# Scale and shift of k tile 0 by one-column matmuls, and silu of c spread by diagonal matmuls, in the prologue of a transformer block

## The chip, the cores and the metric

One Trainium2 chip, of which the kernel uses one core. The metric is the device time of one execution in microseconds (us), the median of three runs.

## The reference

One encoder block on 256 tokens of width 2048, in float32. A modulation vector of 9 x 2048 numbers is computed from c. It scales, shifts and gates three sublayers: a SwiGLU feed-forward (width 5632), a two-headed-group attention, and a second feed-forward.

```
def modulate(n, shift, scale):
    return n * (1 + scale[:, None, :]) + shift[:, None, :]

mod = jax.nn.silu(c) @ w_ada[l] + b_ada[l]            # 2048 x 18432
sh1, sc1, gt1, sh2, sc2, gt2, sh3, sc3, gt3 = jnp.split(mod, N_MOD, axis=-1)
f = swiglu(modulate(rms_norm(h, g_ffn1[l]), sh1, sc1), w1_gate[l], w1_up[l], w1_down[l])
h = h + 0.5 * gt1[:, None, :] * f
... attention with sh2, sc2, gt2, then a second feed-forward with sh3, sc3, gt3
```

## The kernel before

Activations are kept transposed: 16 k tiles (`h[k]`, 128 features by 256 tokens). The weights stream through once, in units of 128x1024 float32 (512 KB, tile `rw`, four buffers). ScalarE rounds a unit to float32r (`hiw`, line 83), VectorE subtracts to get the rest (`low`, line 90), and TensorE makes each product from three matmuls, hi by hi, hi by low and low by hi (lines 222 to 224). The normalised activation of a k tile is split in the same way into `nh` (line 307, ScalarE) and `nl` (line 310, VectorE), after line 304 (VectorE, `nt`) has multiplied h by the row's scale and by 1/rms.

The modulation numbers are made on VectorE. For 128 of them, `ada_use` (line 195) multiplies two 128x1024 units of `w_ada` (tile `ra`) by `cb`, which is silu(c) spread over all 128 partitions, and sums along the row. So one k tile's scale and shift take four such instructions. `acc` holds the results.

The program is written in a fixed order (a manual schedule), and each engine takes its instructions in that order. All loads are issued by SyncE, at most eight under way.

The first stage, `up_start`, runs k tiles 0, 1 and 2 (K1 = 3). Before each k tile, `before1` writes the work that it needs: the four `ada_use`, the norm (lines 304, 307, 310), and the hi and low of two weight units. Each k tile then has 24 matmuls of 512 columns into eight PSUM banks (tile `pa`). From then on `up_pass` takes the rest of the feed-forward, with one weight unit to each twelve matmuls (tile `pu`), and the remaining modulation work is given out at a set rate per unit.

Ahead of `up_start` stand: the load of c, spread over the partitions by the DMA (`cb`, two halves, lines 466 and 468), and of small vectors (`vec`); tanh and one VectorE operation on each half of `cb` for silu (lines 489 and 490); the loads of `ra` for k tile 0, then of x (line 480), then of weights and of `ra` for k tiles 1 and 2; the squares of x (line 503, ScalarE, four of 128x1024); sixteen matmuls of 256 columns with a matrix of ones, which sum the squares over the partitions (line 505, tile `pstat`, plain float32); and 1/rms from that sum (lines 244 to 252, `rs`).

Of the kernel before, what the change touches and what calls it, by code (L numbers as in the profile page):

```python
# [9 lines left out]
F32 = mybir.dt.float32  # L10
F32R = mybir.dt.float32r
AF = mybir.ActivationFunctionType
ALU = mybir.AluOpType
AX = mybir.AxisListType

P = 128
S = 256
D = 2048
KT = D // P
# [6 lines left out]
CW = 1024  # L26
# [123 lines left out]
def build(tc, a):  # L150
    nc = tc.nc
    with ExitStack() as ctx:
        cp = ctx.enter_context(tc.tile_pool(name="cp", bufs=1))
# [4 lines left out]
        def bank(nm):  # L158
            return pb.tile([P, 512], F32, tag="b", name=nm)
# [4 lines left out]
        fl = Flow(tc, a, wp, srcs)  # L164

        ones = cp.tile([P, P], F32, name="ones")
# [3 lines left out]
        ident = cp.tile([P, P], F32, name="ident")  # L170
        make_identity(nc, ident)

        G1, GO, BA = 0, 48, 80
        vec = cp.tile([P, 224], F32, name="vec")
        cb = cp.tile([P, D], F32, name="cb")
        h4 = [cp.tile([P, 4, S], F32, tag=f"h{k}", name=f"h{k}") for k in range(4)]
        h = [h4[k // 4][:, k % 4, :] for k in range(KT)]
        acc = cp.tile([P, 9, 2, KT], F32, name="acc")
# [3 lines left out]
        gsc = cp.tile([P, 3, KT], F32, name="gsc")  # L182
        gin = cp.tile([P, 3, KT], F32, name="gin")
        gat = cp.tile([P, 2, KT], F32, name="gat")

        def ada_use(j, k, b, raw):
            if j in (1, 4, 7):
                scale, init = gsc[:, j // 3, k : k + 1], gin[:, j // 3, k : k + 1]
            elif j in (2, 8):
                scale, init = 0.25, gat[:, j // 3 // 2, k : k + 1]  # L190
            else:
                scale, init = 0.5, vec[:, BA + j * KT + k : BA + j * KT + k + 1]
            if b == 1:
                init = acc[:, j, 0, k : k + 1]
            nc.vector.tensor_tensor_reduce(  # L195
                out=raw, in0=raw, in1=cb[:, b * CW : (b + 1) * CW], scale=scale, scalar=init,
                op0=ALU.mult, op1=ALU.add, accum_out=acc[:, j, b, k : k + 1])
            if b == 1:
                modded.add((j, k))

        modded = set()
# [34 lines left out]
        def ln_exp_set():  # L236
            nc.scalar.preload_act_table_set("natural_log_exp_and_others")

        def rstd_tiles(w, tag):
            ts = [sp.tile([P, S], F32, tag="nt", bufs=4, name="rt")[:, :w] for i in range(2)]  # L240
            return ts + [sp.tile([P, w], F32, tag=tag, bufs=2, name=tag)]

        def rstd_act(ps, n, ts):
            nc.scalar.activation(ts[0], ps, AF.Ln, scale=1.0 / n, bias=epst)
            nc.scalar.activation(ts[2], ts[0], AF.Exp, scale=-0.5)

        def rstd_dve(ps, n, ts):
            t0, t1, r = ts
            nc.vector.tensor_scalar(t1, ps, -0.5 / n, -0.5 * EPS, ALU.mult, ALU.add)
            nc.vector.tensor_tensor(t0, r, r, ALU.mult)  # L250
            nc.vector.tensor_tensor(t0, t0, t1, ALU.mult)
            nc.vector.scalar_tensor_tensor(r, t0, 1.5, r, ALU.add, ALU.mult)
            return r
# [67 lines left out]
        def norm_now(k, r, jsc, jsh):  # L321
            for p in norm_parts(k, r, jsc, jsh):
                p()
# [139 lines left out]
        def big(nm):  # L463
            return hp.tile([P, 8, S], F32, tag="hid", name=nm)

        nc.sync.dma_start(cb[:, :CW], a["c"][0].partition_broadcast(P))
        nc.sync.dma_start(vec, a["vecs"])
        nc.sync.dma_start(cb[:, CW:], a["c"][1].partition_broadcast(P))
        early = {}

        def early_load(k):
            for j in (1, 0):
                t = big("ra")
                for b in range(2):
                    early[k, j, b] = t[:, 4 * b : 4 * b + 4, :].rearrange("p a s -> p (a s)")
                    nc.sync.dma_start(early[k, j, b], a["w_ada"][j * KT + k, b])

        early_load(0)
        for q in range(4):
            nc.sync.dma_start(h4[q], a["x"][q])  # L480
        fl.fetch(1)
        for k in range(1, K1):
            early_load(k)
            fl.fetch(min(2 * k + 1, RAWW - 1))
        thc = big("thc")
        for b in range(2):
            th = thc[:, 4 * b : 4 * b + 4, :].rearrange("p a s -> p (a s)")
            cs = slice(b * CW, (b + 1) * CW)
            nc.scalar.activation(th, cb[:, cs], AF.Tanh, scale=0.5)
            nc.vector.scalar_tensor_tensor(cb[:, cs], th, 1.0, cb[:, cs], ALU.add, ALU.mult)  # L490
        ln_exp_set()
        bias3 = vec[:, BA : BA + 9 * KT].rearrange("p (n j k) -> p n j k", n=3, j=3)
        gains = vec[:, G1 : G1 + 3 * KT].rearrange("p (n k) -> p n k", n=3)
        nc.vector.tensor_scalar(gsc, gains, 0.5, None, ALU.mult)
# [3 lines left out]
        ps1 = bank("pstat")[:, :S]  # L498
        for q in range(4):
            if q % 2 == 0:  # L500
                sq8 = big("sq1")
            sq = sq8[:, 4 * (q % 2) : 4 * (q % 2) + 4, :]
            nc.scalar.activation(sq, h4[q], AF.Square)
            for i in range(4):
                nc.tensor.matmul(ps1, ones, sq[:, i, :], start=q + i == 0, stop=q + i == 6)
        rt = rstd_tiles(S, "rs")

        def early_use(k):
            for j in (1, 0):
                for b in range(2):  # L510
                    ada_use(j, k, b, early[k, j, b])

        mod_jobs(range(K1, KT), 1, 0, rt[2])
        ada_jobs([(j, k) for j in (2, 4, 3, 5) for k in range(KT)])
        mod_jobs(range(SPLIT2[0]), 7, 6)

        def before1(k, j):
            if j == 0:
                early_use(k)
                if k == 0:  # L520
                    rstd_act(ps1, D, rt)
                    rstd_dve(ps1, D, rt)
                norm_now(k, rt[2], 1, 0)
                if k == K1 - 1:
                    fl.top_up()
            if k == K1 - 1:
                return fl.step()
            fl.to_hi(fl.u)
            fl.to_lo(fl.u)
            fl.u += 1  # L530
            return fl.hi.pop(fl.u - 1), fl.lo.pop(fl.u - 1)

        up_start(hp, K1, before1)
        fl.pace(RATE_A)
        up_pass(hp, 2, 0, K1, "first")
# [13 lines left out]
        with tc.tile_pool(name="att", bufs=2) as ap_, tc.tile_pool(name="atc", bufs=1) as ac:  # L549
# [244 lines left out]
            for n in range(len(units)):  # L794
# [13 lines left out]
                u = fl.u  # L808
# [31 lines left out]
def _consts():  # L840
# [21 lines left out]


_SHAPES = {
    "x": (4, P, 4, S), "w_ada": (9 * KT, 2, P, CW), "vecs": (P, 224), "c": (2, CW),
    "w1_s": (SPLIT1[0] * 2, P, CW), "w1_a": ((FT - 8) * 2 * SPLIT1[0] // 8, P, CW),
    "w1_b": (FT * 2 * (SPLIT1[1] - SPLIT1[0]) // 8, P, CW),
    "w1_c": (FT * 2 * (SPLIT1[2] - SPLIT1[1]) // 8, P, CW), "w1_d": (KT * FT // 8, P, CW),
# [8 lines left out]
def _arrays(inputs):  # L877
    g = {k: np.asarray(v) for k, v in inputs.items()}
    rope, lnc, nam, idx = _consts()
    c = np.ascontiguousarray  # L880

    def vec(v):
        return np.asarray(v).reshape(-1, P).T

    wq = g["w_qkv"][0].reshape(8, 2, P, 3, 4, 512).transpose(4, 3, 0, 2, 1, 5).reshape(4, 3, 8, P, CW)
    arr = {
        "x": c(g["x"][0].T.reshape(4, 4, P, S).transpose(0, 2, 1, 3)),
        "w_ada": c(g["w_ada"][0].reshape(2, CW, 9 * KT, P).transpose(2, 0, 3, 1)),
        "vecs": c(np.concatenate([
            vec(g["g_ffn1"][0]), vec(g["g_mix"][0]), vec(g["g_ffn2"][0]),  # L890
            vec(g["g_out_na"][0]), vec(g["g_out_dil"][0]), vec(g["c"][0]), vec(g["b_ada"][0])], axis=1)),
        "qkg": c(np.stack([g["qn_na"][0], g["kn_na"][0], g["qn_dil"][0], g["kn_dil"][0]])),
        "rope": rope, "lnc": lnc, "nam": nam,
        "nab": c(g["rpb_na"][0].reshape(8, -1)[:, idx].reshape(8, 2, P, S).transpose(0, 2, 1, 3)),
        "w_qkv": c(np.stack([wq[g_, j, k_] for g_, j, k_ in QKV_ORDER])),
        "w_o": c(g["w_o"][0].reshape(2, 8, P, KT, P).transpose(0, 3, 2, 1, 4).reshape(2 * KT, P, CW)),
    }

    def stream(blocks):
        return c(blocks.reshape(-1, 8, P, P).transpose(0, 2, 1, 3).reshape(-1, P, CW))  # L900

    def halves(units):
        return c(units.reshape(-1, 2, P, 512).transpose(0, 2, 1, 3).reshape(-1, P, CW))

    arr["c"] = c(g["c"].reshape(2, CW))
    for l, cuts in ((1, SPLIT1), (2, SPLIT2)):
        gu = np.stack([g[f"w{l}_gate"][0], g[f"w{l}_up"][0]]).reshape(2, KT, P, FT // 4, 512)
        gu = gu.transpose(3, 0, 1, 2, 4)
        arr[f"w{l}_s"] = halves(gu[:2, :, : cuts[0]].transpose(2, 0, 1, 3, 4))
        arr[f"w{l}_a"] = halves(gu[2:, :, : cuts[0]])  # L910
        arr[f"w{l}_b"] = halves(gu[:, :, cuts[0] : cuts[1]])
        arr[f"w{l}_c"] = halves(gu[:, :, cuts[1] :])
        arr[f"w{l}_d"] = stream(g[f"w{l}_down"][0].reshape(FT, P, KT, P).transpose(2, 0, 1, 3))
    return arr
# [22 lines left out]
```

## Time and profile before

| | us |
|---|---|
| median of 3 runs (1939.54 to 1940.45) | 1940.07 |
| time of the profiled execution | 1940.19 |
| its span in the trace | 1938.2 |
| TensorE busy in the span | 1894.9 |
| VectorE busy | 1537.9 |
| ScalarE busy | 889.5 |

The profiled execution is 0.12 us above the median, and 1.99 us of its time lie outside the span of the trace. Times in the trace count from the start of the span. PE is TensorE's matmuls, PEld its weight loads, DVE is VectorE, ACT is ScalarE, SPq the issue of loads by SyncE. One float32 matmul of the program appears as two records on PE and two on PEld.

### The profile page before, as it was taken

The numbers are of one execution on the slowest core, as the hardware profiler recorded it, in microseconds if no ns is written. First come the engines' busy times: TensorE is split into PE (matmuls) and PEld (weight loads), VectorE is DVE, ScalarE is ACT, GpSimd is POOL, SyncE is SP. The second block draws the span as 40 slices with busy tenths as digits, with TensorE's granted clock in tenths as the row PEclk, the third lists the DMA queues.
The fourth block names the chain that finished last, engine by engine and source line by source line (L and its number), as shares of the span: only waits on it lengthen the run. The fifth ranks groups of instructions, "written<-read, shape, count | busy, mean of one in ns | idle before, by whom it ended". The sixth has DMA issues, their size and how long they took to land.

```text
span 1938.2 us, 25880 instructions
## 1 busy us (share of the span) xinstructions
PE 1894.9 (98%) x9504; PEld 1604.2 (83%) x9504; DVE 1537.9 (79%) x2106; ACT 889.5 (46%) x1211; POOL 0.7 (0%) x6
## 2 busy tenths in 40 slices
PE   5999999999999999999999998999999999999999
PEld 3888888888888888788888998888888888888887
DVE  5889988888899898778787988777777888876444
ACT  3654444444443333455555544654344544433332
POOL 0000000000000000000000000000000000000000
PEclk9999999999999999999999999999999999999999
DMA  8898887777799999576766656988887766687663
GB/s 315 321 347 305 315 298 246 242 254 259 242 336 350 354 355 352 198 246 209 248 205 208 207 180 201 310 309 277 269 275 264 218 218 219 221 286 245 195 196 125
DMA packets 141104, 504.94 MB, mean 261 GB/s; under 512 B 15665, under 2 KB 17969, under 8 KB 140977
## 3 DMA queue, kind: packets, MB, share of 16 engines
q1 hardware_dynamic: 140976, 503.30, 76.4%
q8 instruction: 74, 1.21, 0.2%
q14 instruction: 54, 0.43, 0.1%
HBM read 501.14 MB, written 2.10 MB: 260 GB/s over the span
## 4 chain that ended last, share of the span: by engine, by line
PE 93%; DVE 5%; DMA 1%; issue 1%; ACT 0%; SPq 0%; DVEq 0%; ACTq 0%
PE pd L227 17%; PE pu L222 16%; PE pu L224 16%; PE pu L223 16%; PE pd L228 9%; PE pqv L222 2%; DVE low L90 2%; PE pqv L223 2%; PE pqv L224 2%; PE pqk L222 2%; PE pqq L222 2%; PE pqk L224 2%; PE pqk L223 2%; PE pqq L224 2%; PE pqq L223 2%; PE ph L383 1%
## 5 line engine op out<-in xcount | busy, mean ns | idle before, releaser
L83 ACT CAST hiw<-rw 128x1024 fp32r<-128x1024 f32 x656 | 692.0, 1056 | 976.4 <-PE pu L224 452.2
L90 DVE TENSOR_TENSOR low<-rw,hiw 128x1024 fp32r<-128x1024 f32 x656 | 801.7, 1223 | 341.1 <-issue 127.6
L222 PE MATMUL pu<-hiw,nx 128*128 128x512 f32 x1352 | 527.8, 390 | 0.0
L224 PE MATMUL pu<-hiw,nx 128*128 128x512 f32 x1352 | 526.3, 389 | 0.0
L223 PE MATMUL pu<-low,nx 128*128 128x512 f32 x1352 | 526.1, 389 | 0.0
L227 PE MATMUL pd<-hd,hiw 128*128 128x512 f32 x1408 | 497.8, 397 | 0.0
L228 PE MATMUL pd<-hd,low 128*128 128x256 f32 x1408 | 395.6, 281 | 0.0
L227 PEld LDWEIGHTS pd<-hd,hiw 128*128 128x128 f32 x1408 | 264.7, 188 | 65.2
L224 PEld LDWEIGHTS pu<-hiw,nx 128*128 128x128 f32 x1352 | 253.8, 188 | 52.9
L223 PEld LDWEIGHTS pu<-low,nx 128*128 128x128 f32 x1352 | 253.8, 188 | 52.3
L222 PEld LDWEIGHTS pu<-hiw,nx 128*128 128x128 f32 x1352 | 253.8, 188 | 52.0
L228 PEld LDWEIGHTS pd<-hd,low 128*128 128x128 f32 x1408 | 264.3, 188 | 0.1
L195 DVE CUSTOM_DVE_ANT_0 ra<-ra,cb,acc 128x1024 f32<-128x1024 f32 x144 | 187.0, 1299 | 0.2
L351 DVE TENSOR_TENSOR pt<-pt,pu 128x512 f32<-128x512 f32 x176 | 112.4, 680 | 0.0
L195 DVE CUSTOM_DVE_ANT_0 ra<-ra,cb,vec 128x1024 f32<-128x1024 f32 x64 | 81.8, 1279 | 0.0
L222 PE MATMUL pso<-ox,hiw 128*128 128x256 f32 x256 | 73.8, 288 | 0.0
L223 PE MATMUL pso<-ox,hiw 128*128 128x256 f32 x256 | 73.1, 286 | 0.0
L224 PE MATMUL pso<-ox,low 128*128 128x256 f32 x256 | 73.1, 286 | 0.0
L195 DVE CUSTOM_DVE_ANT_0 ra<-ra,cb,gin 128x1024 f32<-128x1024 f32 x48 | 64.3, 1339 | 0.0
L222 PE MATMUL pqv<-hiw,nx 128*128 128x512 f32 x128 | 51.5, 402 | 3.4 <-ACT nx L307 3.4
L222 PE MATMUL pqk<-hiw,nx 128*128 128x512 f32 x128 | 51.1, 399 | 0.0
L222 PE MATMUL pqq<-hiw,nx 128*128 128x512 f32 x128 | 50.8, 397 | 0.0
(129 smaller groups left out, 1609.2 us busy)
## 6 DMA issues: line engine op xcount, KB each, us to landing
ra<-in_w_ada_dram SPq DMA_DIRECT2D x288, 512.0 KB, 5.0
rw<-in_w_d_dram SPq DMA_DIRECT2D x176, 512.0 KB, 4.6
rw<-in_w_c_dram SPq DMA_DIRECT2D x154, 512.0 KB, 4.3
rw<-in_w_b_dram SPq DMA_DIRECT2D x121, 512.0 KB, 4.8
rw<-in_w_qkv_dram SPq DMA_DIRECT2D x96, 512.0 KB, 3.8
rw<-in_w_a_dram SPq DMA_DIRECT2D x63, 512.0 KB, 4.9
rw<-in_w_o_dram SPq DMA_DIRECT2D x32, 512.0 KB, 3.5
rw<-in_w_s_dram SPq DMA_DIRECT2D x14, 512.0 KB, 4.6
```

The lines of the kernel that those rows point to most:

```text
L83: self.nc.scalar.copy(t, self.raw[self.nhi])
L90: self.nc.vector.tensor_tensor(t, self.raw.pop(self.nlo), self.hi[self.nlo].bitcast(F32), ALU.subtract)
L195: nc.vector.tensor_tensor_reduce(out=raw, in0=raw, in1=cb[:, b * CW : (b + 1) * CW], scale=scale, scalar=init, op0=ALU.mult, op1=ALU.add, ...
L222: nc.tensor.matmul(out, lh, rh, start=first, stop=False, **kw)
L223: nc.tensor.matmul(out, lh, rl, start=False, stop=False, **kw)
L224: nc.tensor.matmul(out, ll, rh, start=False, stop=last, **kw)
L227: nc.tensor.matmul(ps, lh, r.rearrange("p t s -> p (t s)"), start=first, stop=False)
L228: nc.tensor.matmul(ps[:, :S], ll, r[:, 0, :], start=False, stop=last)
L351: nc.vector.tensor_tensor(part[G][:, j, t, :], part[G][:, j, t, :], ps[t], ALU.add)
L383: nc.tensor.transpose(box[i][:, f, t * P : (t + 1) * P], pt[:, 0, t, cs], ident)
```

## The change

Scale and shift of k tile 0 are no longer made by VectorE. A new input `w_zero` holds the 2048x128 columns of `w_ada` for the scale and those for the shift, laid out as matmul weights. 32 float32 matmuls, each with 128x128 of it as weights and one column of silu(c) as the moving operand, sum up into two columns of a PSUM tile (`pm`). Two VectorE operations of 128x1 turn them into the entries of `acc`.

silu(c) is now taken on a 128x16 copy of c that already lies in `vec` (`sc2`). The spread form `cb`, which the other modulation work still needs, is made by four diagonal matrices (`dg`, identity times a column, VectorE), four float32 matmuls of 512 columns with ones (`pc`), and four ScalarE copies out of PSUM. The broadcast loads of c go. x is loaded ahead of `w_zero`.

The squares of x are added in pairs by VectorE, so that 8 matmuls with ones are left of 16. In `before1` the hi of a weight unit now stands ahead of the norm and its low between lines 304 and 310; before, both stood behind the norm.

```
-        nc.sync.dma_start(cb[:, :CW], a["c"][0].partition_broadcast(P))
         nc.sync.dma_start(vec, a["vecs"])
-        nc.sync.dma_start(cb[:, CW:], a["c"][1].partition_broadcast(P))
...
-        early_load(0)
         for q in range(4):
             nc.sync.dma_start(h4[q], a["x"][q])
+        zero = [eighths("wz") for i in range(2)]
+        for i in range(2):
+            for b in range(2):
+                nc.sync.dma_start(zero[i][b], a["w_zero"][i, b])
...
-            nc.scalar.activation(th, cb[:, cs], AF.Tanh, scale=0.5)
-            nc.vector.scalar_tensor_tensor(cb[:, cs], th, 1.0, cb[:, cs], ALU.add, ALU.mult)
+        nc.scalar.activation(sc2, cc, AF.Tanh, scale=0.5)
         ln_exp_set()
+        nc.vector.scalar_tensor_tensor(sc2, sc2, 1.0, cc, ALU.add, ALU.mult)
+        pcs = [bank("pc") for q in range(4)]
+        for q in range(4):
+            dg = eighths("dg")[0][:, :512].rearrange("p (a b) -> p a b", a=4)
+            nc.vector.tensor_tensor(
+                dg, ident.unsqueeze(1).broadcast_to([P, 4, P]),
+                sc2[:, 4 * q : 4 * q + 4].unsqueeze(2).broadcast_to([P, 4, P]), ALU.mult)
+            nc.tensor.matmul(pcs[q], ones, dg.rearrange("p a b -> p (a b)"), start=True, stop=True)
...
             nc.scalar.activation(sq, h4[q], AF.Square)
-            for i in range(4):
-                nc.tensor.matmul(ps1, ones, sq[:, i, :], start=q + i == 0, stop=q + i == 6)
+            nc.vector.tensor_tensor(sq[:, 0:2, :], sq[:, 0:2, :], sq[:, 2:4, :], ALU.add)
+            for i in range(2):
+                nc.tensor.matmul(ps1, ones, sq[:, i, :], start=q + i == 0, stop=q + i == 4)
+        for q in range(3):
+            nc.scalar.copy(cb[:, q * 512 : (q + 1) * 512], pcs[q])
...
+        rstd_act(ps1, D, rt)
+        nc.scalar.copy(cb[:, 3 * 512 :], pcs[3])
+        rstd_dve(ps1, D, rt)
+        pm = bank("pm")
+        for i in range(2):
+            for c in range(KT):
+                nc.tensor.matmul(
+                    pm[:, i : i + 1], zero[i][c // 8][:, c % 8 * P : (c % 8 + 1) * P], sc2[:, c : c + 1],
+                    start=c == 0, stop=c == KT - 1)
+        nc.vector.tensor_scalar(
+            acc[:, 1, 1, 0:1], pm[:, 0:1], gsc[:, 0, 0:1], gin[:, 0, 0:1], ALU.mult, ALU.add)
+        nc.vector.tensor_scalar(
+            acc[:, 0, 1, 0:1], pm[:, 1:2], 0.5, vec[:, BA : BA + 1], ALU.mult, ALU.add)
...
             if j == 0:
-                early_use(k)
-                norm_now(k, rt[2], 1, 0)
+                if k:
+                    for i in (1, 0):
+                        for b in range(2):
+                            ada_use(i, k, b, early[k, i][b])
+                fl.to_hi(u)
+                p0, p1, p2 = norm_parts(k, rt[2], 1, 0)
+                p0()
+                p1()
+                fl.to_hi(u + 1)
+                fl.to_lo(u)
+                p2()
+                fl.to_lo(u + 1)
```

Three places show how the order of instructions on an engine changes. The first is TensorE's, from its first instruction to the first matmul of the feed-forward (`pa`); rows with - are of before, rows with + of the change, and lines 512 and 505 are the same matmul with ones.

```order
-L505 MATMUL pstat<-sq_151,ones 128x256 x8
-L505 MATMUL pstat<-sq_162,ones 128x256 x8
-L222 MATMUL pa_176<-hiw,nx_85 128x512
...
+L497 MATMUL pc<-dg,ones 128x512 x4
+L512 MATMUL pstat<-sq_163,ones 128x256 x4
+L512 MATMUL pstat<-sq_172,ones 128x256 x4
+L522 MATMUL pm<-sc_138,wz 128x1 x32
+L222 MATMUL pa_229<-hiw,nx_85 128x512
```

Four matmuls now stand ahead of the sums of squares, and 32 one-column ones between these sums and the feed-forward.

The second is VectorE's, at the start of k tile 0 (the same difference stands at k tiles 1 and 2; L195 are the `ada_use` of the next k tile).

```order
 L304 SCALAR_TENSOR_TENSOR nt<-h_80,acc,rs 128x256
+L90 TENSOR_TENSOR low<-rw,hiw 128x1024
 L310 SCALAR_TENSOR_TENSOR nx_85<-nt,acc,nx_85 128x256
-L90 TENSOR_TENSOR low<-rw,hiw 128x1024 x2
+L90 TENSOR_TENSOR low<-rw,hiw 128x1024
 L195 ISA ra,acc<-ra,cb,gin,gsc 128x1024
 L195 ISA acc 128x1
```

One of the two lows has moved up between the norm's two VectorE operations.

The third is the order of loads on SyncE, up to the weights of the first k tile.

```order
-L466 DMA cb<-in_c_dram 128x1024
-L467 DMA vec<-in_vecs_dram 128x224
-L468 DMA cb<-in_c_dram 128x1024
-L476 DMA ra<-in_w_ada_dram 128x1024 x4
-L480 DMA h_80<-in_x_dram 128x1024
...
+L470 DMA vec<-in_vecs_dram 128x224
+L472 DMA h_80<-in_x_dram 128x1024
...
+L476 DMA wz<-in_w_zero_dram 128x1024 x4
 L76 DMA rw<-in_w_s_dram 128x1024 x2
```

Six loads of 512 KB stood ahead of x, and none does now; ahead of the weights the two loads of c are gone.

## Rows read from the trace of the kernel before

**Rows 1.** TensorE's waits over the whole span: total us, times, longest.

```profile
PE pstat L505 <- ACT sq L503: 15.5, 1, 15.5
PE pa L222 <- ACT hiw L83: 7.0, 2, 4.4
```

**Rows 2.** Stretches (us): busy us of PE, PEld, DVE, ACT, POOL; granted clock, DMA share, GB/s.

```profile
25.00:30.00 5.00, 0.50 (x1) 0.19 (x1) 3.83 (x8) 2.81 (x4) 0.00 (x0) 0.95 1.03 411
30.00:35.00 5.00, 4.88 (x12) 3.81 (x13) 4.96 (x8) 0.00 (x0) 0.00 (x0) 0.50 0.93 350
...
49.80:53.40 3.60, 3.60 (x10) 2.78 (x10) 1.82 (x3) 0.78 (x1) 0.00 (x0) 0.53 0.80 257
...
60.00:200.00 140.00, 140.00 (x620) 115.91 (x619) 126.53 (x166) 75.32 (x97) 0.00 (x0) 1.00 0.92 333
```

**Rows 3.** Timelines of the engines, 15 to 31 us: start, us, instruction, times, idle before.

```profile
15.47 9.01 PE L505 MATMUL pstat<-sq,ones 128*128 128x256 f32 x32 [15.47 <-ACT sq L503]
...
16.06 1.91 PE L505 MATMUL pstat<-sq,ones 128*128 128x256 f32 x4
...
19.78 1.46 PE L505 MATMUL pstat<-sq,ones 128*128 128x256 f32 x6
...
18.22 1.06 ACT L503 ACTIVATE sq<-h 128x1024 f32<-128x1024 f32 x1 [0.24 <-DMA h<-in_x_dram]
...
24.52 0.47 ACT L244 ACTIVATE rt<-pstat,epst 128x256 f32<-128x256 f32 x1 [5.24 <-PE pstat L505]
...
26.85 0.48 DVE L304 SCALAR_TENSOR_TENSOR nt<-h,acc,rs 128x256 f32<-128x256 f32 x1
28.85 2.36 DVE L90 TENSOR_TENSOR low<-rw,hiw 128x1024 fp32r<-128x1024 f32 x2 [0.45 <-DMA ra<-in_w_ada_dram]
31.12 1.34 DVE L195 CUSTOM_DVE_ANT_0 ra<-ra,cb,gin 128x1024 f32<-128x1024 f32 x1
```

**Rows 4.** The same, 36 to 50 us, VectorE and TensorE.

```profile
36.31 0.48 DVE L304 SCALAR_TENSOR_TENSOR nt<-h,acc,rs 128x256 f32<-128x256 f32 x1
40.58 1.34 DVE L195 CUSTOM_DVE_ANT_0 ra<-ra,cb,gin 128x1024 f32<-128x1024 f32 x1
45.77 0.48 DVE L304 SCALAR_TENSOR_TENSOR nt<-h,acc,rs 128x256 f32<-128x256 f32 x1
...
44.74 0.39 PE L224 MATMUL pa<-hiw,nx 128*128 128x512 f32 x1
47.78 0.50 PE L222 MATMUL pa<-hiw,nx 128*128 128x512 f32 x1 [2.65 <-ACT hiw L83]
49.05 0.50 PE L223 MATMUL pa<-low,nx 128*128 128x512 f32 x1 [0.76 <-DVE low L90]
49.38 0.40 PE L224 MATMUL pa<-hiw,nx 128*128 128x512 f32 x1
```

**Rows 5.** The first issue of a load (timeline); then KB and us from issue to landing.

```profile
0.74 0.39 SPq L466 DMA_DIRECT2D cb<-in_c_dram  x1
...
vec<-in_vecs_dram SPq DMA_DIRECT2D x1, 112.0 KB, 4.2
```

**Rows 6.** TensorE records with small shapes: min/median/max ns of lines, and timeline rows.

```profile
L383 PEld LDWEIGHTS ph<-ident,pt x176: 137/141/143, 306.3 to 1690.8; 128*128 128x128 f32 x176
L383 PE MATMUL ph<-ident,pt x176: 270/273/331, 306.3 to 1690.9; 128*128 128x128 f32 x176
...
867.11 0.38 PE L693 MATMUL pT<-ident,kn 128*128 128x128 f32 x2
...
781.71 0.30 PEld L292 LDWEIGHTS pstat<-sq,ones 128*128 128x128 f32 x2 [1.53 <-DVE sq L271]
...
L292 PEld LDWEIGHTS pstat<-sq,ones x8: 186/190/190, 781.7 to 1189.4; 128*128 128x128 f32 x8
```

**Rows 7.** VectorE groups of 128x512 and 128x16: busy us, mean ns.

```profile
L686 DVE TENSOR_TENSOR nab<-nab,nam 128x512 f32<-128x512 f32 x8 | 5.5, 682 | 0.0
L497 DVE TENSOR_SCALAR gat<-vec 128x16 f32<-128x16 f32 x2 | 0.2, 166 | 0.0
```

More of the change, by code (lines that the diff above doesn't have):

```diff
@@ L171, in build @@
         make_identity(nc, ident)
-        G1, GO, BA = 0, 48, 80
+        G1, GO, CC, BA = 0, 48, 64, 80
         vec = cp.tile([P, 224], F32, name="vec")
@@ L464, in big, with eighths @@
             return hp.tile([P, 8, S], F32, tag="hid", name=nm)
-        nc.sync.dma_start(cb[:, :CW], a["c"][0].partition_broadcast(P))
+        def eighths(nm):
+            t = big(nm)
+            return [t[:, 4 * b : 4 * b + 4, :].rearrange("p a s -> p (a s)") for b in range(2)]
         nc.sync.dma_start(vec, a["vecs"])
-        nc.sync.dma_start(cb[:, CW:], a["c"][1].partition_broadcast(P))
[L469 to L476, printed above, removed]
@@ L478, in build @@
-        early_load(0)
         for q in range(4):
             nc.sync.dma_start(h4[q], a["x"][q])
+        zero = [eighths("wz") for i in range(2)]
+        for i in range(2):
+            for b in range(2):
+                nc.sync.dma_start(zero[i][b], a["w_zero"][i, b])
         fl.fetch(1)
+        early = {}
         for k in range(1, K1):
-            early_load(k)
+            for j in (1, 0):
+                early[k, j] = eighths("ra")
+                for b in range(2):
+                    nc.sync.dma_start(early[k, j][b], a["w_ada"][j * KT + k, b])
@@ L484, in build @@
             fl.fetch(min(2 * k + 1, RAWW - 1))
[L485 to L488, printed above, removed]
-            nc.scalar.activation(th, cb[:, cs], AF.Tanh, scale=0.5)
-            nc.vector.scalar_tensor_tensor(cb[:, cs], th, 1.0, cb[:, cs], ALU.add, ALU.mult)
-        ln_exp_set()
+        cc = vec[:, CC : CC + KT]
+        sc2 = cp.tile([P, KT], F32, name="sc2")
+        nc.scalar.activation(sc2, cc, AF.Tanh, scale=0.5)
@@ L503, in build @@
             nc.scalar.activation(sq, h4[q], AF.Square)
-            for i in range(4):
-                nc.tensor.matmul(ps1, ones, sq[:, i, :], start=q + i == 0, stop=q + i == 6)
-        rt = rstd_tiles(S, "rs")
[L508 to L511, printed above, removed]
+            nc.vector.tensor_tensor(sq[:, 0:2, :], sq[:, 0:2, :], sq[:, 2:4, :], ALU.add)
[3 more added lines that the diff above has]
+            nc.scalar.copy(cb[:, q * 512 : (q + 1) * 512], pcs[q])
+        rt = rstd_tiles(S, "rs")
+        rstd_act(ps1, D, rt)
[11 more added lines that the diff above has]
+            acc[:, 0, 1, 0:1], pm[:, 1:2], 0.5, vec[:, BA : BA + 1], ALU.mult, ALU.add)
+        modded.update({(1, 0), (0, 0)})
         mod_jobs(range(K1, KT), 1, 0, rt[2])
@@ L517, in before1 @@
         def before1(k, j):
+            u = fl.u
             if j == 0:
-                early_use(k)
-                if k == 0:
-                    rstd_act(ps1, D, rt)
-                    rstd_dve(ps1, D, rt)
-                norm_now(k, rt[2], 1, 0)
+                if k:
+                    for i in (1, 0):
+                        for b in range(2):
+                            ada_use(i, k, b, early[k, i][b])
[7 more added lines that the diff above has]
+                fl.to_lo(u + 1)
                 if k == K1 - 1:
@@ L527, in before1 @@
                 return fl.step()
-            fl.to_hi(fl.u)
-            fl.to_lo(fl.u)
             fl.u += 1
-            return fl.hi.pop(fl.u - 1), fl.lo.pop(fl.u - 1)
+            return fl.hi.pop(u), fl.lo.pop(u)
         up_start(hp, K1, before1)
@@ L864 @@
 _SHAPES = {
-    "x": (4, P, 4, S), "w_ada": (9 * KT, 2, P, CW), "vecs": (P, 224), "c": (2, CW),
+    "x": (4, P, 4, S), "w_ada": (9 * KT, 2, P, CW), "vecs": (P, 224), "w_zero": (2, 2, P, CW),
     "w1_s": (SPLIT1[0] * 2, P, CW), "w1_a": ((FT - 8) * 2 * SPLIT1[0] // 8, P, CW),
@@ L903, in halves @@
         return c(units.reshape(-1, 2, P, 512).transpose(0, 2, 1, 3).reshape(-1, P, CW))
-    arr["c"] = c(g["c"].reshape(2, CW))
+    arr["w_zero"] = c(np.stack([
+        g["w_ada"][0][:, j * D : j * D + P].reshape(2, 8, P, P).transpose(0, 2, 1, 3).reshape(2, P, CW)
+        for j in (1, 0)]))
     for l, cuts in ((1, SPLIT1), (2, SPLIT2)):
```

## The prediction

> **What bounds the kernel now.** I read TensorE's waits first. Over the whole span its longest wait is the first one, 15.5 us until the first square of x is there; after it come 7.0 us in two waits for a hi in the first stage [rows 1]. Then I read the stretches: from 60 to 200 us TensorE is busy for all of 140.00 us, while VectorE has 126.53 and the loads run at 333 GB/s, less than the 411 that they reached at 25 to 30 us [rows 2]. So from about 50 us on TensorE sets the pace, its work there is not touched by the change, and the whole question is how much earlier its unbroken work begins. I take as mark the third matmul of k tile 2, line 224 at 49.38 us [rows 4], since by then nh, nl, hi and low are all there and nothing more is waited for.
>
> What leads to the mark is a chain. Sixteen float32 matmuls with ones run 9.01 us from 15.47 [rows 3]. The reader should see two rates in them: the four records from 16.06 take 1.91 us, three steps of 0.43 and a last record of 0.63; the six from 19.78 take 1.46, five steps of 0.216 and a last one of 0.38 [rows 3]. The clock rose from its lower level (1.2 GHz) to the upper (2.4 GHz) about 4 us after TensorE had begun. 1/rms follows, and line 304 of k tile 0 starts at 26.85; the next k tile's `ada_use` start at 31.12 and 40.58, and line 304 of k tiles 1 and 2 at 36.31 and 45.77 [rows 3, 4]. Between the two 304s VectorE has a period of 9.46 us, and TensorE waits for it: its last matmul of k tile 1 starts at 44.74 and its next at 47.78 [rows 4].
>
> **The change, part by part.** I work out when `pm` is done, then follow VectorE to the mark.
>
> *c.* `vec` is now the first load. It took 4.2 us to land [rows 5], so issued at 0.74 like the first load before [rows 5] it is there at 4.9. The tanh and the silu on 128x16 I put at 0.2 us each, as the 128x16 operation took 0.166 [rows 7]; the first diagonal follows at 5.3 and takes 0.68 like other operations of 128x512 [rows 7]. `pc` begins at 6.0. The other three diagonals, one each 0.68, come faster than TensorE uses them.
>
> *pc.* A 128x256 float32 matmul is two records, 0.86 us at the lower level and 0.43 at the upper [rows 3]; 512 columns cost twice that, 1.72 and 0.86. With the rise 4 us after the start, 4.0/1.72 = 2.33 of the four are done by 10.0, and the other 1.67 take 1.44: done at 11.4. If the clock rises later the bound is 4 x 1.72 = 6.9, done at 12.9.
>
> *Squares.* 3.15 MB less stand ahead of the last quarter of x (six units of 0.524 MB); at 411 GB/s [rows 2] that is 7.7 us. The last square started at 18.22 [rows 3], so it starts at about 10.5, ends at 11.6, and VectorE's addition of 0.68 ends at 12.3. TensorE, which comes free at 11.4, takes 8 x 0.43 = 3.45 us for the four pairs and so begins the last pair at 14.0: the loads of x are no longer what it waits for. The sums are done at 14.9. 1/rms behind them takes 26.85 - 24.52 = 2.33 us [rows 3], until about 17.3, and is hidden beside `pm`, as are the four copies of `cb` on ScalarE. `w_zero` lands behind x, 2.1 MB at 411 GB/s, from about 10.4 to 15.5; its last quarter is used last, so it hides too.
>
> *pm*, the disputed price. 32 matmuls make 64 records, each with a weight load of 128 columns and one column to move. No row has that. The nearest is the pair of loads at line 292, which start 0.30 - 0.19 = 0.11 us apart, far from the start with the clock up; the pair of 128-column matmuls at line 693 (records as long as line 383's, 0.27) stands 0.38 - 0.27 = 0.11 apart too, loads included [rows 6]. I take 0.11: 64 x 0.11 = 7.0 us, done at 21.9. From below: if in those pairs the load and the 128 columns took turns, the load alone is half, 0.055, 3.5 us. From above: if nothing overlapped, a load of 0.141 and a matmul of 0.27 [rows 6] make 0.41, 26.2 us.
>
> A page of the Trainium skill, "TensorE: Matmul & The Clock Gate", section "Back-to-back issue gap", gives about 81 ns for a sustained pair of load and matmul at 128 columns. By it `pm` would be an estimated 5.2 us and the gain 1.8 us more than my sum. The rows here have 0.11 for a pair, and I go by them; the same page, under "Weight-path perf modes", says that the fast weight load is off for FP32, which these weights are.
>
> *From pm to the mark.* In four terms:
> - Two operations of 128x1 and the waits around them, 0.4 us (0.17 each by the 128x16 row [rows 7], bounds 0.2 and 0.6). Line 304 of k tile 0 starts at 22.3 and not 26.85: **4.5 us**.
> - From line 304 to the next `ada_use` it was 31.12 - 26.85 = 4.27 [rows 3]. VectorE waited there for nh, and 0.45 more before the lows [rows 3]. Now a low stands where it waited for nh, with its hi made before. Left are line 304 (0.48, I take 0.45, since what follows overlaps its end as the second low does), line 310 (0.40), the two lows (2.36) and 0.1 for the second hi, 3.3: **1.0 us**.
> - The same at k tile 1, 40.58 - 36.31 = 4.27 [rows 4]: **1.0 us**. The `ada_use` themselves stay (36.31 - 31.12 = 5.19). The four of k tile 0 that go save nothing by themselves: VectorE did them while TensorE worked on the squares.
> - At k tile 2, from line 304 to the mark, it was 49.38 - 45.77 = 3.61 [rows 4]. Now the mark waits for 304, low (half of 2.36) and 310: 0.45 + 1.18 + 0.40 + 0.1 = 2.1: **1.5 us**. Line 224 now waits for nl behind low, where it waited for low alone; this is in the sum.
>
> Sum 8.0 us. Cover: the loads of `ra` for k tile 1 come 1.05 MB (2.6 us) earlier than before, and VectorE asks for them 5.5 us earlier (31.12 to 25.6). Before, the last `ra` of k tile 2 was there by 35 us (DMA busy 0.93 of 30 to 35, 1.03 ahead of it [rows 2]); now that is by about 32.4, and it is asked for at 22.3 + 3.3 + 5.2 + 3.3 + 3.9 = 38.0 (three quarters of the 5.2). So they still hide.
>
> One term more is the clock. Before, it stood at the lower level (0.53) from 49.80 to 53.40 [rows 2], behind TensorE's idle 2.8 us and another 0.8. That cost 3.60 x (1 - 0.53) = 1.7 us. The idle time ahead of k tile 2 becomes shorter, but k tile 1 is done earlier too; I can't say whether the clock falls and count half, 0.8. At k tile 0, where the clock was low before (granted 0.50 at 30 to 35 us [rows 2]), a lower clock costs nothing: 24 matmuls of 0.43 take 10.3 us, from 24.4 to 34.7, the 24 of k tile 1 at the upper level (140.00/620 = 0.226 each [rows 2]) then 5.4, to 40.1, and the mark is not before 41.4.
>
> Forecast: 8.8 us. The profiled execution took 1940.19, 0.12 above the median; 1940.19 - 8.8 = 1931.4, and by the median 1931.3.
>
> **The rivals.**
> *pm is cheaper.* With 0.055 each record `pm` ends at 18.4, and 3.5 us more are won: 1927.8. For it speaks that the moving column is one and not 128; against it, that the two loads of line 292 stand 0.11 apart, the second with only the first ahead of it [rows 6].
> *The clock falls during pm.* One column of each record leaves the array nearly without work, so the clock may go to its lower level, as it did when TensorE had idled 4.4 us ahead of k tile 0 (granted 0.95, then 0.50 [rows 1, 2]). A record then costs twice 0.11. If half of the 64 pay it, `pm` takes 10.5, if all do 14.1; the gain is 5.3 to 1.7: 1934.8 to 1938.4. Against it: TensorE has worked densely for 9 us before.
> *Slower.* Successive records add to the same PSUM column, and if each waits for the one before, a record costs up to 0.41 and `pm` 26.2, ending at 41.1; the gain of 8.8 becomes a loss of 10.4: 1950.5. It decides from 0.11 + 8.8/64 = 0.25 us each record. Against it speaks that the records of line 505 follow each other each 0.216 us, though one lasts 0.38 and all add to one tile [rows 3].
> *The lead is lost later*, because loads or VectorE hold the steady part back: 1940. Against it: no idle time of TensorE from 60 to 200 us, and loads below their peak [rows 2].
>
> **How the numbers follow.** Forecast 0.55 (1929 to 1934), pm cheaper 0.12, clock falls 0.15, slower 0.12, lost 0.06. The predicted time is the forecast's. A measurement of this kernel can tell about 0.2%, 3.9 us. Faster: 0.55 + 0.12 and a little over half of the clock's case, 0.76. Same: the rest of it and the lost lead, 0.12. Slower: 0.12. The range goes from the cheap pm, 1927, to the far end of the clock's case, 1938.5; outside lie the slower case and most of the lost lead.
>
> **What the changed profile should show.** `pc` from about 6 to 11.4, the sums of squares done by 15, `pm` as 64 records with a step of 0.11 and its end at 22; line 304 of k tile 0 at 22.3; the `ada_use` of k tiles 1 and 2 starting at 25.6 and 34.1; the mark at 41.4, 8.0 before 49.38; then no idle time of TensorE that before did not have. The prediction is wrong if the step of `pm` is above 0.2, if VectorE's period stays at 9.4, or if the lead at the mark is not there at 200 us.

## The result: slower, and the profile after

| | before | after |
|---|---|---|
| median, 20 runs each | 1940.06 us (1938.92 to 1942.12) | 1943.26 us (1938.57 to 1956.93) |
| ratio | | 1.0023, 95% interval 1.0013 to 1.0032 |
| profiled execution, span | 1940.19, 1938.2 us | 1956.93, 1955.2 us |

The change made the kernel slower by 0.23% by the ratio of the mean times; the medians lie 3.2 us apart, 0.16%. The spread is a result too: before lies within 3.2 us, after within 18.4, and the profiled execution of after is the longest of its 20. That the other runs have a smaller part of what its trace shows is an inference from their times, since they have no trace.

I read the start first: is the lead there that the prediction is made of? VectorE and TensorE of after, start, us, instruction, times:

```profile
2.82 0.22 ACT L488 ACTIVATE sc<-vec 128x16 f32<-128x16 f32 x1 [0.80 <-DMA vec<-in_vecs_dram]
...
4.09 6.59 PE L497 MATMUL pc<-dg,ones 128*128 128x512 f32 x8 [4.09 <-DVE dg L494]
...
10.52 3.62 PE L512 MATMUL pstat<-sq,ones 128*128 128x256 f32 x16
...
13.97 11.09 PE L522 MATMUL pm<-sc,wz 128*128 128x1 f32 x64
...
25.43 0.47 DVE L304 SCALAR_TENSOR_TENSOR nt<-h,acc,rs 128x256 f32<-128x256 f32 x1
...
33.75 0.48 DVE L304 SCALAR_TENSOR_TENSOR nt<-h,acc,rs 128x256 f32<-128x256 f32 x1
...
42.09 0.48 DVE L304 SCALAR_TENSOR_TENSOR nt<-h,acc,rs 128x256 f32<-128x256 f32 x1
...
43.16 0.50 PE L222 MATMUL pa<-hiw,nx 128*128 128x512 f32 x1 [2.02 <-ACT nx L307]
...
44.15 0.80 PE L224 MATMUL pa<-hiw,nx 128*128 128x512 f32 x1
```

It is: line 304 of k tile 0 starts 1.4 us earlier than before (26.85), its period is 8.3 us in place of 9.46, and the mark is at 44.15 in place of 49.38 [rows 3, 4]. The lead at the mark is 5.2 us. Yet the span is 17.0 us longer, so 22.2 us are lost behind the mark.

Where? The prediction named the row to look at: TensorE from 60 us on. Stretches of after, TensorE alone (us, busy us and records, granted clock, DMA share, GB/s):

```profile
60.00:200.00 140.00, 140.00 (x602) 1.00 0.92 328
200.00:300.00 100.00, 100.00 (x430) 1.00 0.85 291
1250.00:1350.00 100.00, 100.00 (x431) 1.00 0.87 293
1350.00:1450.00 100.00, 100.00 (x430) 1.00 0.81 261
```

The same stretches of before, as far as [rows 2] lack them:

```profile
200.00:300.00 100.00, 100.00 (x443) 1.00 0.88 300
1250.00:1350.00 100.00, 100.00 (x443) 1.00 0.88 296
1350.00:1450.00 100.00, 100.00 (x443) 1.00 0.83 271
```

TensorE is busy without a gap in both, at a granted clock of 1.00 in both, and starts fewer matmuls: 602 against 620 in 140 us [rows 2]. Its step, the time from one start to the next, went from 140/620 = 0.2258 to 140/602 = 0.2326 us. From 60 to 200 us after falls 18 matmuls behind, 4.1 us of the 5.2; to 300 us it is 31, 7.0 us, more than the lead. The prediction's third sign of being wrong, a lead that is not there at 200 us, is met but for 1.1 us. A share of 100% hides it: "busy" says that a record is open, not how fast the next follows. The costliest groups of after (busy us, mean ns, idle ahead) show it summed up:

```profile
L222 PE MATMUL pu<-hiw,nx 128*128 128x512 f32 x1352 | 537.3, 397 | 0.0
...
L224 PE MATMUL pu<-hiw,nx 128*128 128x512 f32 x1352 | 534.6, 395 | 0.0
L223 PE MATMUL pu<-low,nx 128*128 128x512 f32 x1352 | 533.2, 394 | 0.0
```

Before, they were these:

```profile
L222 PE MATMUL pu<-hiw,nx 128*128 128x512 f32 x1352 | 527.8, 390 | 0.0
L224 PE MATMUL pu<-hiw,nx 128*128 128x512 f32 x1352 | 526.3, 389 | 0.0
L223 PE MATMUL pu<-low,nx 128*128 128x512 f32 x1352 | 526.1, 389 | 0.0
```

No idle time in either; together 24.9 us more, for the same 4056 instructions with the same operands. (The ends of records are modelled, so this sum need not be the 22.2 exactly.)

### The profile page after: what moved, and what is told of

Its sections match the earlier page's. It is cut to its first block, busy times and chain, and to the rows that moved or that the text cites. A ratio compares the mean times of both kernels' runs of the same rounds, so it can differ in the third digit from the quotient of the medians.

```text
span 1955.2 us, 25990 instructions
## 1 busy us (share of the span) xinstructions
PE 1928.5 (99%) x9560; PEld 1617.1 (83%) x9560; DVE 1537.7 (79%) x2107; ACT 889.3 (45%) x1214; POOL 0.7 (0%) x6
## 4 chain that ended last, share of the span: by engine, by line
PE 93%; DVE 5%; DMA 1%; issue 1%; SPq 0%; ACT 0%; DVEq 0%
PE pd L227 17%; PE pu L222 16%; PE pu L224 16%; PE pu L223 16%; PE pd L228 9%; PE pqv L222 2%; PE pqv L224 2%; PE pqv L223 2%; PE pqk L223 2%; PE pqk L224 2%; PE pqq L223 2%; PE pqk L222 2%; PE pqq L224 2%; PE pqq L222 2%; DVE low L90 1%; PE ph L383 1%
## 5 line engine op out<-in xcount | busy, mean ns | idle before, releaser
L222 PE MATMUL pu<-hiw,nx 128*128 128x512 f32 x1352 | 537.3, 397 | 0.0
L224 PE MATMUL pu<-hiw,nx 128*128 128x512 f32 x1352 | 534.6, 395 | 0.0
L223 PE MATMUL pu<-low,nx 128*128 128x512 f32 x1352 | 533.2, 394 | 0.0
L224 PEld LDWEIGHTS pu<-hiw,nx 128*128 128x128 f32 x1352 | 254.9, 189 | 59.7
L195 DVE CUSTOM_DVE_ANT_0 ra<-ra,cb,acc 128x1024 f32<-128x1024 f32 x142 | 184.6, 1300 | 0.1
L195 DVE CUSTOM_DVE_ANT_0 ra<-ra,cb,vec 128x1024 f32<-128x1024 f32 x63 | 80.6, 1280 | 0.0
L224 PE MATMUL pso<-ox,low 128*128 128x256 f32 x256 | 72.8, 285 | 0.0
L195 DVE CUSTOM_DVE_ANT_0 ra<-ra,cb,gin 128x1024 f32<-128x1024 f32 x47 | 63.0, 1341 | 0.0
L222 PE MATMUL pqv<-hiw,nx 128*128 128x512 f32 x128 | 51.6, 403 | 3.5 <-ACT nx L307 3.5
L224 PE MATMUL pqv<-hiw,nx 128*128 128x512 f32 x128 | 51.0, 399 | 0.0
```

Source lines behind the costliest of these rows:

```text
L195: nc.vector.tensor_tensor_reduce(out=raw, in0=raw, in1=cb[:, b * CW : (b + 1) * CW], scale=scale, scalar=init, op0=ALU.mult, op1=ALU.add, ...
L222: nc.tensor.matmul(out, lh, rh, start=first, stop=False, **kw)
L223: nc.tensor.matmul(out, lh, rl, start=False, stop=False, **kw)
L224: nc.tensor.matmul(out, ll, rh, start=False, stop=last, **kw)
```

## The experiments

**The theory.** What differs for these matmuls is where their operands lie. The change allocates `sc2`, 16 floats or 64 bytes a partition, in the pool `cp` behind the other constants. The pools of the weight units (`rw`, `hiw`, `low`) and all that is allocated after them move up by 64 bytes; the activations `nx`, allocated ahead of it, do not. In lines 222 to 224 `nx` is the weights and `hiw` or `low` the moving operand. Worked out from the tile sizes, `hiw` lay 49,664 bytes behind `nx` before, 194 times 256, and lies 64 bytes more behind it now. All buffers and column slices of the two are multiples of 256 bytes apart, so every one of these matmuls has the same distance modulo 256.

The theory says that the step depends on the distance between moving operand and weights. Its rivals: the changed start itself (other order of VectorE's work, other phase of the loads) slows the steady part; or the place of the weight units matters by itself, and not the distance. All kernels but e7 alter only where tiles lie (and clear, once, the unused bytes of a pad); every one computes all of the reference.

**e1: the change, with `sc2` in unused space of `acc`.** The start is as in after, the addresses as before. If the start is at fault, the step stays at 0.2326.

```
-        sc2 = cp.tile([P, KT], F32, name="sc2")
+        sc2 = acc[:, 8, 0, :]
```

> The changed kernel, with its 128x16 tile sc2 laid into an unused part of acc, so that no other tile of SBUF moves; the instructions are the same. Theory A (addresses): the slower step of the feed-forward matmuls (0.229 and 0.233 us where before had 0.2267) comes from the 64 bytes by which sc2 shifts the weight tiles against the activations; here the step is 0.2267 everywhere and the time is before less the lead at the mark, 1940.1 - 5.3 = 1934.8, with a spread of some 2 us. Theory B (prologue): the step is set by what TensorE does at the start (one-column matmuls, banks taken in another order, the clock's rises); here it is slow as in the change, 1940 to 1957.

Measured 1934.43 us (1930.74 to 1935.78; before beside it 1940.14), ratio 0.9968, interval 0.9955 to 0.9981. Its profiled execution took 1931.33. One stretch of e1, TensorE alone:

```profile
60.00:200.00 140.00, 140.00 (x619) 1.00 0.93 335
```

And its timelines:

```profile
12.69 9.24 PE L522 MATMUL pm<-acc,wz 128*128 128x1 f32 x64
...
22.29 0.48 DVE L304 SCALAR_TENSOR_TENSOR nt<-h,acc,rs 128x256 f32<-128x256 f32 x1
30.61 0.48 DVE L304 SCALAR_TENSOR_TENSOR nt<-h,acc,rs 128x256 f32<-128x256 f32 x1
38.94 0.48 DVE L304 SCALAR_TENSOR_TENSOR nt<-h,acc,rs 128x256 f32<-128x256 f32 x1
...
41.00 0.50 PE L224 MATMUL pa<-hiw,nx 128*128 128x512 f32 x1
```

The step of before is back, and in this execution the whole lead arrives at the end: 8.4 us at the mark, 8.9 in time. By the medians the gain is 5.7 us. The changed start is not what slowed the matmuls.

**e2: before, with 64 unused bytes.** The other half: the old start, the new addresses.

```
         gat = cp.tile([P, 2, KT], F32, name="gat")
+        pad = cp.tile([P, KT], F32, name="pad")
+        nc.vector.memset(pad, 0.0)
```

> The kernel before, with an unused 128x16 tile (64 bytes a partition, one memset) at the same place as sc2, so that the weight tiles and all behind them lie 64 bytes higher. Theory A: the matmul step rises to 0.229 or 0.233 in the feed-forward and the projections and the time to 1945 to 1960, spread over several us. Theory B: step 0.2267 and 1940.1 as before.

Measured 1950.67 us (1949.73 to 1957.57), ratio 1.0059 (1.0045 to 1.0072). TensorE's stretches of e2:

```profile
60.00:200.00 140.00, 140.00 (x601) 1.00 0.92 323
200.00:300.00 100.00, 100.00 (x430) 1.00 0.86 295
1250.00:1350.00 100.00, 100.00 (x439) 1.00 0.88 300
```

64 bytes that nothing reads make before slower by 10.5 us in the median, 11.4 in the mean. The last row shows the second thing: at the same distance the step has two values, 100/430 = 0.2326 and 100/439 = 0.2278, and one run has both. After's profiled execution has 430 and 431 in its late stretches too, and is the longest of 20. That the two values come in other shares from run to run fits the spread of after, which before and e1 don't have; only one run of each kernel has a trace, so it is not shown. An estimate agrees with it: at 0.2278 throughout, the 4224 up matmuls (tiles `pu` and `pa`) would cost 4224 x 0.0020 = 8.4 us, and after's fastest run, 1938.57, is 7.8 above the fastest of e1.

**e3: the change with 128 bytes.**

```
-        sc2 = cp.tile([P, KT], F32, name="sc2")
+        sc2 = cp.tile([P, 2 * KT], F32, name="sc2")[:, :KT]
```

> The changed kernel with sc2 as 128x32 of which half is used, so that the weight tiles lie 128 bytes higher than before and not 64. Theory A, if only the place within 128 bytes counts: step 0.2267 and 1934.8. Theory A, if any shift counts: slow as the change. Theory B: slow as the change, 1940 to 1957.

Measured 1959.67 us (1956.04 to 1962.16), ratio 1.0098 (1.0085 to 1.0111). Its stretches:

```profile
60.00:200.00 140.00, 140.00 (x602) 1.00 0.93 328
1250.00:1350.00 100.00, 100.00 (x430) 1.00 0.87 293
```

Here the slow step stands in the late stretch too, so a shift by 128 bytes is no cure. e3 starts like e1 (`pm` of 8.92 us, k tile 2 at 40.01 in both) and takes 1960.4 - 1931.33 = 29.1 us longer. The 4056 matmuls of `pu` and 168 of `pa` at 0.2326 - 0.2258 = 0.0068 would give 28.7. That this is so near is chance. The attention's projections, which run on the same lines with the same two operands, also lose: from the first `pqv` record to the last of `pqq` e1 takes 292.5 us and e3 298.2, 5.7 more. And e3 wins 1.5 us behind the mark, where its clock stays up (shown in the next section). So 30.6 us are to explain, and the terms give 34.4: the slow step accounts for the loss, but not every matmul pays the whole of 0.0068.

**e4, e5, e8: distance or place?** Edits to e1. e4 moves `gsc` and `gat` (320 bytes) ahead of `nx` and puts 64 unused bytes behind it: the distance is 256 less. e5 allocates `sc2` ahead of `nx`: both operands move up by 64, the distance is that of before. e8 moves `gsc` alone (192 bytes) and adds 128 bytes behind: the distance is 64 less.

e4, with `nx` allocated between the two pieces:

```
+        gsc = cp.tile([P, 3, KT], F32, name="gsc")
+        gat = cp.tile([P, 2, KT], F32, name="gat")
...
-        gsc = cp.tile([P, 3, KT], F32, name="gsc")
-        gat = cp.tile([P, 2, KT], F32, name="gat")
+        pad = cp.tile([P, KT], F32, name="pad")
+        nc.vector.memset(pad, 0.0)
```

e5, the first line ahead of `nx`:

```
+        sc2 = cp.tile([P, KT], F32, name="sc2")
...
-        sc2 = acc[:, 8, 0, :]
```

e8, again around `nx`:

```
+        gsc = cp.tile([P, 3, KT], F32, name="gsc")
...
-        gsc = cp.tile([P, 3, KT], F32, name="gsc")
+        pad = cp.tile([P, 2 * KT], F32, name="pad")
+        nc.vector.memset(pad, 0.0)
```

> The changed kernel with sc2 in acc and with two small tiles moved ahead of the activations and 64 bytes of padding behind them: activations 320 bytes and weight tiles 64 bytes higher than before, so the distance between the two is 256 bytes less. Before, that distance is a multiple of 512. Theory A1 (only the distance within 256 bytes counts): step 0.2267, time as with no shift, 1934.4. Theory A2 (within 512 bytes or more): slow step of 0.229 or more, 1940 to 1960. Theory A3 (the weight tiles' own place counts, 64 bytes off): slow as well.

> The changed kernel with sc2 allocated ahead of the activations, so that activations and weight tiles both lie 64 bytes higher than before and their distance is that of before. Theory A1, A2 (the distance counts): step 0.2267, 1934.4. Theory A3 (the weight tiles' own place counts): slow as the change, 1940 to 1957.

> The changed kernel with sc2 in acc, with one small tile (192 bytes) moved ahead of the activations and 128 bytes of padding behind them, so that the distance of the weight tiles to the activations is 64 bytes less than a multiple of 256, where in the change it is 64 more. If every distance that is no multiple of 256 costs: step 0.229 to 0.2335 in the feed-forward, 1943 to 1960. If only some do: 0.2267 and 1931 to 1935.

| kernel | distance to before's, bytes | records, 60 to 200 us | median us (range) | ratio to before, 95% |
|---|---|---|---|---|
| e4 | -256 | 619 | 1931.17 (1929.69 to 1933.85) | 0.9961, 0.9948 to 0.9973 |
| e5 | 0, both moved by 64 | 619 | 1933.82 (1929.47 to 1935.05) | 0.9965, 0.9952 to 0.9977 |
| e8 | -64 | 602 | 1964.14 (1962.5 to 1966.56) | 1.0124, 1.0109 to 1.014 |

Neither operand's own place matters: in e5 `hiw` lies where it lies in after, and the step is the fast one. The distance does, and a whole 256 bytes of it does not. One rival is left. `rw`, which the loads fill, moves with `hiw` and `low` in every one of these edits, so a collision of TensorE's reads with the writes of other engines has no edit of its own; against it speaks that after keeps its 0.2326 at a DMA share of 0.92 and of 0.81. (e8's profiled execution is 3.9 us longer than e3's at the same count of records: 2.6 of it are there by the first `pqv` record, with a clock that fell behind the mark in e8 and not in e3, and 1.3 lie in `pso`.)

**e6, e9: the same rule where before breaks it.** In the down projections (lines 227 and 228) `hiw` and `low` are the weights and the activations `hd` move. By the sizes their distance is 64 bytes short of a multiple of 256, in before and in after. A gap of 64 bytes ahead of each of the two pools of `hd` mends it: e6 is e1 with the gaps, e9 is before with them.

```
+        hps.enter_context(tc.tile_pool(name="gap1", bufs=1)).tile([P, 16], F32, name="gap")
...
+        ctx.enter_context(tc.tile_pool(name="gap2", bufs=1)).tile([P, 16], F32, name="gap")
```

> The changed kernel with sc2 in acc, and 64 bytes of padding ahead of the pool of the hidden activations, which are the moving operand of the down projections; their distance to the weight tiles (there the weights) then is a multiple of 256 bytes, where it was 64 off in every kernel so far. In the down projections a pair of matmuls (512 and 256 columns) steps 0.2350 + 0.1185 = 0.3535 us. If the distance counts there too: 0.3467 (two times 13.3 ns above the columns), 1408 pairs, 9.6 us less, 1925. If it does not: 1934.4.

> The kernel before with 64 bytes of padding ahead of the pool of the hidden activations and nothing else. If the gain of e6 over e1 is the address alone: 1408 pairs of matmuls at 0.3467 and not 0.3535, 9.6 us less than before, 1930.4. If it needs the changed prologue: 1940.

e6: 1923.38 us (1922.01 to 1925.19), ratio 0.9917 (0.9904 to 0.9931). e9: 1930.12 us (1929.17 to 1930.85), ratio 0.9948 (0.9935 to 0.996). A stretch of down projections in before:

```profile
560.00:760.00 200.00, 200.00 (x1134) 1.00 0.96 356
```

The same in e6:

```profile
560.00:760.00 200.00, 200.00 (x1156) 1.00 0.97 361
```

A pair of 512 and 256 columns went from 400/1134 = 0.3527 to 400/1156 = 0.3460 us; 1408 pairs at 0.0067 make 9.4 us, and the profiled executions of e1 and e6 differ by 1931.33 - 1922.01 = 9.3. That these agree to a tenth is luck: another 1.5 us of the 9.3 lie in `pso`, the attention's output projection (106.7 us from first to last record in e1, 105.2 in e6). e9 against before, without the changed start, gives the same size, 10.1 us by the medians. e6 beats both kernels.

**e7: what the moved lows are worth.** e1 with the norm, the his and the lows in the order of before.

```
+                norm_now(k, rt[2], 1, 0)
                 fl.to_hi(u)
-                p0, p1, p2 = norm_parts(k, rt[2], 1, 0)
-                p0()
-                p1()
-                fl.to_hi(u + 1)
                 fl.to_lo(u)
-                p2()
+                fl.to_hi(u + 1)
                 fl.to_lo(u + 1)
```

> The changed kernel with sc2 in acc, and hi and low of the weight units behind the norm again as before, one thing undone. By the prediction's terms the lows' move is worth 1.0 + 1.0 + 1.5 us, so the mark comes 3.5 us later than at 41.0 and the time is 1938; if VectorE's waits there were hidden, 1934.4.

Measured 1936.35 us (1932.89 to 1939.22), ratio 0.9983 (0.9974 to 0.9992). Its timelines:

```profile
25.41 0.47 DVE L304 SCALAR_TENSOR_TENSOR nt<-h,acc,rs 128x256 f32<-128x256 f32 x1
34.86 0.48 DVE L304 SCALAR_TENSOR_TENSOR nt<-h,acc,rs 128x256 f32<-128x256 f32 x1
...
48.19 0.63 PE L224 MATMUL pa<-hiw,nx 128*128 128x512 f32 x1
```

The execution of e5 that was profiled has line 304 of k tile 0 at 25.44 and the mark at 44.20. From the same start e7 comes 4.0 us later to the mark, and its period is the 9.45 us of before. In time the move is worth less: the median of e7 is 1.9 us above e1's and 2.5 above e5's, between the two expected values.

## Why the prediction was wrong

**The step that failed** is the first paragraph's: "on TensorE sets the pace, its work there is not touched by the change". The work there was not touched, but its step was, through an allocation of 64 bytes (e1 and e2). The prediction took the diff's operations as all of the change; the line that creates `sc2` has no cost of its own and was passed over. The rival "the lead is lost later" had the right place for the loss but the wrong cause (loads or VectorE) and a price of nothing beyond the lead. No case held a slower TensorE, so the forecast has no term for it. In numbers: after's median is 12 us above the forecast of 1931.3; with the old addresses (e1) 8.8 of them are gone, and 3.1 are left for the terms below.

**The sum up to the mark** held nearly. With the old addresses (e1) it comes to this:
- *vec* landed 2.1 us after its issue and not 4.2: in after the tanh on it starts at 2.82 and `pc` began at 4.1 (predicted 6.0).
- *pc* took 5.2 us in e1 (predicted 5.4) and 6.6 in after, near the bound of 6.9 for a late rise of the clock. `pstat` followed; that x would not be waited for is right.
- *pm* was mis-sized. 64 x 0.11 = 7.0 became 9.24 in e1 and 11.09 in after. The 0.11 is right as long as the clock is up, and the rival "the clock falls during pm" was at work as well. Stretches of `pm` alone in after, TensorE:

```profile
14.00:16.50 2.50, 2.50 (x24) 1.00 1.03 413
18.00:24.00 6.00, 6.00 (x30) 0.50 1.03 411
```

  24 records in 2.5 us are some 0.11 each, 30 in 6.0 some 0.21, at a granted clock of 0.50, the lower level. So the step doubles when the clock halves, as the rival had it (0.22). By the prediction's own sign (a step above 0.2) this part of `pm` went wrong. The rival's 10.5 (half) to 14.1 (all) enclose after's 11.09; e1 lies below them.

  The Trainium skill, "TensorE: Matmul & The Clock Gate", section "Back-to-back issue gap", gives about 81 ns for a sustained pair of load and matmul at 128 columns. These records, which move one column, took more at either level, 0.11 and 0.21 us.
- *Line 304 of k tile 0* was predicted at 22.3 and came at 22.29 in e1: the early `vec` paid for the slow `pm`. In after both `pc` and `pm` were longer, and it came at 25.43.
- *The lows* were to give 1.0 + 1.0 + 1.5 = 3.5; e7 against e5 has 4.0. The mechanism is right, the period fell from 9.46 to 8.3 as forecast (8.5).
- *The clock behind the mark*: half a spell, 0.8 us, was counted as a gain. In e1 and in after the spell came back. Stretch of e1, from the mark on (busy of PE, PEld, DVE, ACT, POOL):

```profile
41.40:44.80 3.40, 3.40 (x10) 2.66 (x9) 1.89 (x2) 1.39 (x2) 0.00 (x0) 0.50 0.81 199
```

  TensorE still idles 2 us ahead of k tile 2, and the clock fell to 0.50 for 3.4 us, as it did to 0.53 for 3.6 before [rows 2]. In e3 it did not fall, though TensorE idled 1.95 us there and the mark is at 40.99; the same stretch of e3:

```profile
41.40:44.80 3.40, 3.40 (x16) 2.74 (x15) 3.10 (x3) 2.16 (x3) 0.00 (x0) 1.00 0.68 217
```

  The first L224 record of `pu` then starts at 46.69 in e3 and at 48.21 in e1, so the spell costs 1.5 us. To count half of it was fair; what decides whether it comes is open.

So the lead of e1's profiled execution, 8.9 us, is the forecast's 8.8 by terms that partly offset each other. The medians of e1 (1934.43) and e5 (1933.82) are 2.5 to 3 us above the forecast: their runs lie at 1929 to 1931.5 and at 1933.5 to 1936, with none between. The profiled executions of e1 and e4, with a `pm` of 9.2 to 9.3 us, are in the first group; that of e5, with 11.17, is in the second. That the others divide for the same reason is likely, but I have no trace of them, and a spell that comes or not would move them too.

**What stays open.** Why TensorE minds the distance of its two operands, and why at 256 bytes, no run shows. Nor is it shown what picks between the two steps at a distance of +64. No trace prints an address: the distances are worked out from the order and sizes of the allocations.

## What to carry to other kernels

An allocation is a change too: before costing the operations of a diff, see which tiles it moves, and compare the distance of the operands of the hottest matmuls. When a kernel with TensorE at 100% gets slower or faster without a reason, count its records in equal stretches of both traces; the busy share and the waits can't show a changed step. And an A/B comparison of any edit that adds a tile should keep the addresses behind it, or it measures both.

## What the runs showed of the hardware

- The step of back-to-back matmuls (float32r, 128x128 weights, 512 columns, clock granted 1.00) depends on the distance of moving operand and weights modulo 256 bytes. In counts from 60 to 200 us: 619 to 620 at 0 (0.226 us), 601 to 602 at +64, +128 and -64 (0.2326). At +64 a second step of 0.2278 comes in other stretches of the same run.
- The clock fell during a run of one-column float32 matmuls in which TensorE was not idle: in after the granted clock was 1.00 from 14.0 to 16.5 us and 0.50 from 18 to 24, both wholly busy with them.
- A granted clock of 1.00 in a row does not say that records already run at the pace of the upper level. Of the first stretch of after:

```profile
5.00:8.00 3.00, 3.00 (x5) 1.34 (x4) 2.42 (x8) 2.52 (x3) 0.00 (x0) 1.00 1.02 412
```

  It prints 1.00, while `pc`'s eight records of 512 columns took 6.59 us, 0.82 each, where the upper level is worth 0.43 by the records of line 505 for half the columns, twice 0.216 [rows 3].
- A 112 KB load issued as the first of its queue landed after 2.1 us; as the second, behind a load of 512 KB, it had taken 4.2 [rows 5]. Loads of after (KB, us from issue to landing):

```profile
vec<-in_vecs_dram SPq DMA_DIRECT2D x1, 112.0 KB, 2.1
```
